# A two-layer transformer trunk on one core: when first weights, a norm, kept weights and projection steps are issued

## The chip, the core and the metric

The kernel runs on one core of a Trainium2 chip. The core has five engines with an instruction stream each: TensorE (PE, matmuls), VectorE (DVE), ScalarE (ACT), GpSimd (POOL) and SyncE (SP); POOL and SP issue nearly all DMAs here. The metric is the device time of one execution in microseconds (us), given as the median of several runs.

## What is computed

The input x has 512 positions of 1024 values. Two layers, each a token mixer and a feed-forward network (FFN), are added to it in turn, each behind an RMS norm, all in float32:

```python
def stick_breaking_mixer(h, w_in, w_out):            # layer 0: 16 heads of 64
    q, k, v = split(h @ w_in, 3)
    z = q k^T / 8;  earlier = key < query
    log_keep = where(earlier, log_sigmoid(-z), 0)
    weight = where(earlier, exp(log_sigmoid(z) + sum of log_keep of later keys), 0)
    return (weight @ v) @ w_out

def diff_mixer(h, positions, w_in, w_out, ...):      # layer 1: 8 heads, q and k 2 x 64, v 128
    q, k, v = split(h @ w_in, 3)
    q, k = rms_norm(q) * q_g, rms_norm(k) * k_g      # per 64 values
    q1, q2, k1, k2 = partial_rope(...)               # the first 16 of 64 values are turned
    a = softmax(mask(q1 k1^T / 8)) - lam * softmax(mask(q2 k2^T / 8))   # mask: chunks of 64
    o = rms_norm(a @ v) * sub_g * (1 - lam_init)
    return o @ w_out

def swiglu_ffn(h, w_gate, w_up, w_down):             # 2816 hidden values
    return (silu(h @ w_gate) * (h @ w_up)) @ w_down
```

## The kernel before

Activations lie transposed, as eight tiles of 128 features by 512 positions (`x[0]` to `x[7]`). To keep float32 accuracy, each matmul operand is split in a rounded part and a rest (`whi`, `wlo` for weights, `hhi`, `hlo` for activations), and each product is three matmuls (`mm3`, L215 to L218). A weight tile of 128x1024 (512 KB) is loaded raw and split by ACT (L109, rounding copy) and DVE (L110, subtraction); in layer 0 a form `wload_acc` is also used, in which POOL's DMA accumulates the rest (`wlo<-in_wv` in the trace).

`stick_layer` is layer 0. It loads q and k weights of its first pair of heads, splits x, computes `ps_q` and `ps_k` of that pair, then the first V block, and goes through eight pairs of heads. `ffn` (L550) is the FFN, in three groups of hidden blocks `f`: gate (`ps_g`) and up (`ps_u`) projections, silu, and `ps_d` for the way down. The norm's factor per position is not applied to its input but behind the matmuls: `norm.finish` sums squares with four small matmuls (`ps_ss`, L190), takes a root on DVE, and in the FFNs spreads the factor over 128 partitions with a matmul (`ps_bc`) and an ACT copy (`rbc`, L213).

While FFN 0 runs, `keep_split` loads the 32 weight tiles of layer 1, splits them and writes both parts back to HBM by POOL's DMAs ("kept" weights), so that layer 1 only loads them. Before, it is called for each hidden block `f` under 20.

`diff_layer` is layer 1. `norm.finish` is called ahead of its first projection. Then it makes chunk 0 of q and k for two heads (`qk_steps`: `ps_nat` of 512 columns, squares, a root, a multiply of the whole 128x2048 chunk at L745, the rotary turn at L762 to L765), `head_stacks` (transposes `tqk` into operands of a head, the halves of k copied by a POOL DMA), and V of chunk 0. Each of the eight heads then calls `attend`: for query tiles 3, 2, 1, 0 `weights` makes two score tiles (`sc`), ACT writes the mask into a 64x64 corner (L786), DVE takes the maximum (L787), ACT the exponential (L788), DVE combines both maps (L800); `wt_bank` transposes the result (`tp`) and splits it (`wt_hi`, `wt_lo`); then `av` is the product with V. `head_out` normalises a head: transposes `tn`, sums of squares on ACT (L835), a root on DVE, four ACT copies with that factor (L850), transposes back (`tb`), a split (`ohi`, `olo`, L857, L858). `out_first` multiplies heads 0 to 3 by the output weights (`ps_o`), `out_second` heads 4 to 7.

The order on each engine is not written out. A scheduler lists the instructions ahead of time from the program's order, which counts as priority, and from its own estimate of when operands are ready. Projections are put between the parts of a head as generators in a queue, the fillers:

```python
def fill(n):                      # n steps of the first generators in the queue
def attend(...):                  # tiles 3 | after, fill | 2 | middle, fill | 1 | fill | 0 | flush
```

`after` is the output of the head before, `middle` makes the next head's stacks. Before, an even head takes the q/k chunk of the next two heads as its filler, an odd head the V chunk, and head 6 and head 7 `out_first`; `flush` empties the queue at each head's end. PSUM has eight banks; `mm` holds two for projections, `scp` the scores, `tnp` the transposes of `head_out`.

Of the kernel before, what the change touches and what calls it, by code (L numbers as in the profile page):

```python
# [43 lines left out]
def trunk(  # L44
# [190 lines left out]
    def flush():  # L235
        while fillers:
            fill(1)
# [46 lines left out]
    def out_second(layer, og, hook, alt):  # L284
# [13 lines left out]
        ws = [out_load(layer, 1, g) for g in range(2)]  # L298
        for g in range(2):
            part(g, ws[g], range(4, 7), False)  # L300
        for g in range(2):
            part(g, ws[g], range(7, 8), True)
        for g in range(2, 4):
            part(g, out_load(layer, 1, g), range(4, 8), True)
# [63 lines left out]
    def attend(tpp, wts, weigh, after, middle, steps):  # L368
        w = [None] * TT
        w[3] = weigh(3)  # L370
        after()
        fill(steps)
        w[2] = weigh(2)
        wt_bank(tpp, wts, w, (2, 3))
        middle()
        fill(steps)
        w[1] = weigh(1)
        wt_bank(tpp, wts, w, (1,))
        fill(steps)
        w[0] = weigh(0)  # L380
        wt_bank(tpp, wts, w, (0,))
        flush()
# [4 lines left out]
    def stick_layer(norm, nxt):  # L387
        h = norm.h
        with ExitStack() as st:
# [7 lines left out]
            first = [wload(wqk0[0])]  # L397
            for i in range(1, 3):
                nc.sync.dma_start(out=x[i], in_=xT[i])
            first.append(wload(wqk0[8]))  # L400
            for i in range(3, KT):
                nc.sync.dma_start(out=x[i], in_=xT[i])
            nc.sync.dma_start(out=gf, in_=g_ffn)
            for i in range(KT):
                norm.scaled(i)
# [11 lines left out]
            def v_chunk(c):  # L417
# [15 lines left out]
                return v, nat_steps([wload_acc(wv0[c, j]) for j in range(2)], h, evac, 256, 1)  # L433
# [14 lines left out]
            pq = mm.tile([P, S], F32, tag="mm", name="ps_q")  # L448
            pk = mm.tile([P, S], F32, tag="mm", name="ps_k")
# [35 lines left out]
            def head(hd, q2, k2, v, after):  # L485
                e = hd % 2
                attend(tpp, wts, lambda qt: weights(q2, k2, e, qt), after, nothing, 1)
# [32 lines left out]
            after = nothing  # L520
            vn = None
            for p in range(8):
                nq = []
                if p < 7:
                    fillers.append(qk_steps(p + 1, nq))
                else:
                    last = out_first(0, og)
                    fillers.append(islice(last, 4))
                o32 = at.tile([P, S], F32, tag="o32", name="o32")
                av = head(2 * p, q2, k2, v, after)  # L530
                after = partial(av_done, 0, av, o32)
                if p == 7:
                    fillers.append(last)
                elif p < 6:
# [3 lines left out]
                av = head(2 * p + 1, q2, k2, v, after)  # L538
                after = partial(pair_done, av, o32)
                if nq:  # L540
                    q2, k2 = nq
# [3 lines left out]
            banks = [(mm, "mm"), (mm, "mm"), (scp, "sc"), (scp, "sc"), (scp, "sc"), (tpp, "tp")]  # L545
            out_second(0, og, nxt.tile_done, banks)

    def ffn(layer, norm, hook, side=None):
        h = norm.h
        with ExitStack() as st:  # L550
# [4 lines left out]
            for j, (f0, nf) in enumerate(THIRDS):  # L555
                a = []
                for f in range(f0, f0 + nf):
# [19 lines left out]
                    if side is not None and f < 20:  # L577
# [109 lines left out]
    def diff_layer(norm, nxt):  # L687
        h = norm.h
        with ExitStack() as st:
# [12 lines left out]
            neg = sm.tile([P, 1], F32, tag="neg", bufs=1, name="neg")  # L702
            V.memset(neg, NEG)
            corner = neg[0:64].to_broadcast([64, 64])
# [4 lines left out]
            def v_chunk(c):  # L709
# [15 lines left out]
                return (vh, vl), nat_steps([wload_kept(("wv", c, j)) for j in range(2)], h, evac, 256, 1)  # L725

            def qk_steps(c, out):
# [3 lines left out]
                def evac(t, ps):  # L731
                    A.activation(t_[:, t], ps, AF.Copy, scale=norm.rstd[:, t : t + 1])
# [45 lines left out]
            def weights(q2, k2, ss, qt):  # L778
# [26 lines left out]
            def head(hh, q2, k2, v, after, middle, steps):  # L805
                ss = sm.tile([P, 2, TT], F32, tag="s12", name="s12")
                attend(tpp, wts, lambda qt: weights(q2, k2, ss, qt), after, middle, steps)
                av = avp.tile([P, S], F32, tag="av", name="av")
# [12 lines left out]
            def head_out(av, ss):  # L821
# [46 lines left out]
            v, steps = v_chunk(0)  # L868
            fillers.append(steps)
            flush()  # L870
            after = nothing
            for hd in range(8):
                hh = hd % 2
                if hd >= 6:
                    if hd == 6:
                        last = out_first(1, og)
                    fillers.append(islice(last, 4) if hd == 6 else last)
                elif hh == 0:
                    fillers.append(qk_steps(hd // 2 + 1, qk))
                else:  # L880
                    vn, steps = v_chunk(hd // 2 + 1)
                    fillers.append(steps)

                def middle():
                    if hd < 7:
                        stacks.append(head_stacks(qk[(hd + 1) // 2], (hd + 1) % 2))

                q2, k2 = stacks[hd]
                av, ss = head(hh, q2, k2, v, after, middle, 2 if hh == 0 and hd < 6 else 1)
                after = partial(head_out, av, ss)  # L890
                if hh == 1 and hd < 7:
# [93 lines left out]
```

## Time and profile before

| | before |
|---|---|
| median of 3 runs | 1269.38 us (1269.35 to 1270.61) |
| the profiled execution | 1275.86 us, span 1274.1 us |
| granted PE clock, mean over the span | 0.98 of full speed |
| PE busy | 1228.4 us, 96% |
| DVE, ACT, POOL busy | 726.1, 585.1, 80.8 us |
| HBM read, written | 154.36, 35.65 MB |

Durations are read from the one profiled execution, so a sum of them is compared with 1275.86 us, not with the median. An engine's busy time is a share over stages with different limits; what a change in one stage is worth is read from that stage. A matmul of 512 columns follows the one before it after 0.23 us at the full clock and after 0.43 us at half.

### The profile page before, as it was taken

To read this page: it belongs to the slowest core of one execution; us is meant where nothing else is said; L and a number is where in the kernel's file an instruction comes from. 1 tells how busy PE (TensorE), PEld (TensorE's weight loads), DVE (VectorE), ACT (ScalarE), POOL (GpSimd) and SP (SyncE) were. 2 spreads that over 40 slices of the span, in tenths; PEclk is the share of its full clock that TensorE was granted. 3 is DMA by queue.
4 is the path that set the end of the run, shared out by engine and by line. 5 is a ranking of instruction groups with operands and counts; after the bars stand their busy time and mean duration, and the time that the engine had idled before them with its cause. 6 is when DMAs were issued, how large, how long until landed. Compare 5 with 4: busy or idle time off the path is not lost.

```text
span 1274.1 us, 15991 instructions
## 1 busy us (share of the span) xinstructions
PE 1228.4 (96%) x5974; PEld 1032.7 (81%) x5974; DVE 726.1 (57%) x1349; ACT 585.1 (46%) x1054; POOL 80.8 (6%) x132
## 2 busy tenths in 40 slices
PE   6999999899999999999999999997899999999998
PEld 4888988777888888888788998776788888888887
DVE  5577777677654655454624776874664434443442
ACT  7788887455332433243414476754442223321220
POOL 1111111001111111100000000000000000000000
PEclk8999999999999999999999999998899999999999
DMA  8766858257777777774735453530233322333222
GB/s 249 189 146 136 190 125 190 66 172 259 243 237 250 248 229 233 243 237 140 272 121 190 153 193 114 174 100 17 100 116 100 95 94 93 100 100 99 95 75 79
DMA packets 60269, 199.44 MB, mean 157 GB/s; under 512 B 8224, under 2 KB 8224, under 8 KB 60192
## 3 DMA queue, kind: packets, MB, share of 16 engines
q1 hardware_dynamic: 41904, 140.74, 34.1%
q0 software_dynamic: 18144, 57.68, 17.0%
q8 instruction: 47, 0.77, 0.2%
q14 instruction: 30, 0.25, 0.1%
q10 hardware_dynamic: 144, 0.01, 0.0%
HBM read 154.36 MB, written 35.65 MB: 149 GB/s over the span
## 4 chain that ended last, share of the span: by engine, by line
PE 87%; issue 6%; DVE 2%; ACT 2%; DMA 2%; POOL 0%; SPq 0%; ACTq 0%; DVEq 0%; POOLq 0%
PE ps_d L218 6%; PE ps_d L216 6%; PE ps_d L217 6%; PE ps_u L216 6%; PE ps_u L218 6%; PE ps_u L217 6%; PE ps_g L217 6%; PE ps_g L218 6%; PE ps_g L216 6%; PE ps_nat L216 5%; PE ps_nat L217 5%; PE ps_nat L218 5%; PE ps_o L216 2%; PE ps_o L217 2%; PE ps_o L218 2%
## 5 line engine op out<-in xcount | busy, mean ns | idle before, releaser
L109 ACT ACTIVATE whi<-wraw 128x1024 fp32r<-128x1024 f32 (+1 forms) x138 | 140.8, 1033 | 359.5 <-PE ps_d L217 79.2
L110 DVE TENSOR_TENSOR wlo<-wraw,whi 128x1024 fp32r<-128x1024 f32 (+1 forms) x138 | 164.4, 1192 | 92.3 <-ACT whi L109 39.2
L216 PE MATMUL ps_u<-hhi,whi 128*128 128x512 f32 x352 | 138.2, 393 | 4.2 <-DVE k L655 2.2
L218 PE MATMUL ps_u<-hhi,wlo 128*128 128x512 f32 x352 | 138.1, 392 | 0.0
L217 PE MATMUL ps_g<-hlo,whi 128*128 128x512 f32 x352 | 138.1, 392 | 0.0
L217 PE MATMUL ps_u<-hlo,whi 128*128 128x512 f32 x352 | 137.9, 392 | 0.0
L216 PE MATMUL ps_g<-hhi,whi 128*128 128x512 f32 x352 | 137.1, 390 | 0.0
L218 PE MATMUL ps_g<-hhi,wlo 128*128 128x512 f32 x352 | 137.0, 389 | 0.0
L217 PE MATMUL ps_d<-alo,whi 128*128 128x512 f32 x352 | 136.6, 389 | 0.0
L218 PE MATMUL ps_d<-ahi,wlo 128*128 128x512 f32 x352 | 136.6, 389 | 0.0
L216 PE MATMUL ps_d<-ahi,whi 128*128 128x512 f32 x352 | 136.4, 389 | 0.0
L216 PE MATMUL ps_nat<-whi,hhi 128*128 128x256 f32 (+1 forms) x384 | 126.7, 330 | 4.7 <-DVE q L309 4.0
L217 PE MATMUL ps_nat<-wlo,hhi 128*128 128x256 f32 (+1 forms) x384 | 125.3, 326 | 2.4 <-DMA wlo<-in_wv 2.4
L218 PE MATMUL ps_nat<-whi,hlo 128*128 128x256 f32 (+1 forms) x384 | 125.0, 326 | 0.0
L586 DVE TENSOR_TENSOR x<-x,ps_d 128x512 f32<-128x512 f32 x48 | 32.7, 685 | 90.8 <-PE ps_d L218 90.8
L216 PEld LDWEIGHTS ps_nat<-whi,hhi 128*128 128x128 f32 x384 | 74.7, 194 | 11.0 <-issue 4.0
L216 PEld LDWEIGHTS ps_u<-hhi,whi 128*128 128x128 f32 x352 | 66.8, 190 | 18.9 <-issue 2.6
L217 PEld LDWEIGHTS ps_nat<-wlo,hhi 128*128 128x128 f32 x384 | 74.7, 194 | 8.0 <-DMA wlo<-in_wv 2.9
L218 PEld LDWEIGHTS ps_nat<-whi,hlo 128*128 128x128 f32 x384 | 74.6, 194 | 4.9
L217 PEld LDWEIGHTS ps_u<-hlo,whi 128*128 128x128 f32 x352 | 66.8, 190 | 14.1 <-DVE hlo L162 0.3
L218 PEld LDWEIGHTS ps_u<-hhi,wlo 128*128 128x128 f32 x352 | 66.7, 190 | 13.9
L217 PEld LDWEIGHTS ps_g<-hlo,whi 128*128 128x128 f32 x352 | 66.2, 188 | 14.2 <-issue 0.5
(205 smaller groups left out, 2326.7 us busy)
## 6 DMA issues: line engine op xcount, KB each, us to landing
wraw<-in_wgu SPq DMA_DIRECT2D x88, 512.0 KB, 3.6
wraw<-in_wd SPq DMA_DIRECT2D x32, 512.0 KB, 3.5
wraw<-in_wqk SPq DMA_DIRECT2D x16, 512.0 KB, 4.7
k<-k POOLq DMA_DIRECT2D x32, 256.0 KB, 3.3
praw<-in_wqk SPq DMA_DIRECT2D x16, 512.0 KB, 5.6
kept_wqk<-whi POOLq DMA_DIRECT2D x16, 512.0 KB, 4.3
kept_wqk<-wlo POOLq DMA_DIRECT2D x16, 512.0 KB, 6.5
whi<-kept_wqk SPq DMA_DIRECT2D x16, 512.0 KB, 5.9
```

The costliest lines, as they stand in the source:

```text
L109: A.activation(hi[:, :cols], raw[:, :cols], AF.Copy)
L110: V.tensor_tensor(lo[:, :cols], raw[:, :cols], hi.bitcast(F32)[:, :cols], op=ALU.subtract)
L216: T.matmul(ps, lh[0], rh[0], start=first, stop=False)
L217: T.matmul(ps, lh[0], rh[1], start=False, stop=False)
L218: T.matmul(ps, lh[1], rh[0], start=False, stop=last)
L586: V.tensor_tensor(x[m], x[m], ps, op=ALU.add)
```

## The change

It has seven parts:

- Start: q and k weights of the first pair are loaded and split in four quarters of 256 columns, between the x tiles, and `ps_q`, `ps_k` lie in the score banks, not in `mm`.
- Layer 0: `attend` takes a number of filler steps for each of its four places, a V chunk is loaded at its first step, `out_first` and the flushes move.
- `out_second`: three pairs of output tiles are begun ahead of the last head, not two, with two more banks in the list.
- FFN 0: kept weights are split and stored from block 2 on, not in blocks 0 to 19.
- Layer 1's norm is finished inside the first projection block's evacuation (`norm_ready`), in the bank `tn`.
- Layer 1: the mask's corner is a DVE memset, the last factor of `head_out` one DVE multiply.
- Layer 1: the q/k and V chunks 1 to 3 are all put in the queue ahead of head 0 and drawn by a table `counts`; a chunk is flushed only where its result is needed.

```diff
+    def flush(upto=None):
+        while fillers and (upto is None or upto in fillers):
...
-        ws = [out_load(layer, 1, g) for g in range(2)]
+        early = range(3)
+        ws = [out_load(layer, 1, g) for g in early]
...
         after()
-        fill(steps)
+        fill(steps[0])
         w[2] = weigh(2)
         wt_bank(tpp, wts, w, (2, 3))
+        fill(steps[1])
         middle()
-        fill(steps)
         w[1] = weigh(1)
         wt_bank(tpp, wts, w, (1,))
-        fill(steps)
+        fill(steps[2])
         w[0] = weigh(0)
         wt_bank(tpp, wts, w, (0,))
-        flush()
+        fill(steps[3])
...
-            first = [wload(wqk0[0])]
...
+            raws = [raw_tile(), raw_tile()]
+            first = [pair(), pair()]
+            for j in range(4):
+                c = slice(j * 256, (j + 1) * 256)
+                for i, (raw, (hi, lo)) in enumerate(zip(raws, first)):
+                    nc.sync.dma_start(out=raw[:, c], in_=wqk0[8 * i][:, c])
...
+                norm.scaled(2 * j)
+                for raw, (hi, lo) in zip(raws, first):
+                    A.activation(hi[:, c], raw[:, c], AF.Copy)
+                    V.tensor_tensor(lo[:, c], raw[:, c], hi.bitcast(F32)[:, c], op=ALU.subtract)
+                norm.scaled(2 * j + 1)
...
-            pq = mm.tile([P, S], F32, tag="mm", name="ps_q")
-            pk = mm.tile([P, S], F32, tag="mm", name="ps_k")
+            pq = scp.tile([P, S], F32, tag="sc", name="ps_q")
+            pk = scp.tile([P, S], F32, tag="sc", name="ps_k")
...
-                    if side is not None and f < 20:
+                    if side is not None and f > 1:
                         keep_split(rawp, *side[1].pop(0))
...
-            norm.finish(mm, "mm")
-            V.tensor_scalar_mul(rsv, norm.rstd, phi)
+            def norm_ready():
+                if not norm.done:
+                    norm.finish(tnp, "tn")
+                    V.tensor_scalar_mul(rsv, norm.rstd, phi)
...
                 def evac(t, ps):
+                    norm_ready()
...
-                    A.activation(ps[0:64, n - 64 : n], corner, AF.Copy)
+                    V.memset(ps[0:64, n - 64 : n], NEG)
...
-                for t in range(TT):
-                    c = slice(t * P, (t + 1) * P)
-                    A.activation(on[:, c], tp[:, c], AF.Copy, scale=u[:, t : t + 1])
+                V.tensor_tensor(
+                    on.rearrange("p (t d) -> p t d", d=P),
+                    tp.rearrange("p (t d) -> p t d", d=P),
+                    u.unsqueeze(2).to_broadcast([P, TT, P]),
...
+            for c in range(1, 4):
+                gens["qk", c] = qk_steps(c, qk)
+                gens["v", c] = v_steps(c, vs)
+                fillers.extend((gens["qk", c], gens["v", c]))
+            last = out_first(1, og)
+            counts = ((2, 1, 2, 1), (2, 1, 1, 1)) * 3 + ((1, 1, 1, 1), (1, 1, 1, 1))
...
                     if hd < 7:
+                        if hh == 1:
+                            flush(gens["qk", c + 1])
...
+                def before():
+                    if c > 0:
+                        flush(gens["v", c])
+                    if hd == 6:
+                        fillers.append(last)
```

How the listed order moves, at three places (a name's number is its buffer; what an instruction waits for stands in brackets: an engine, `DMAHW` for a load by SP's queue, `DMASW` for a DMA of POOL).

PE, between FFN 0's last matmuls (`ps_d`) and layer 1's first (`ps_nat`), before:

```order
L217 MATMUL ps_d_5586<-alo_5311,whi_5572 128x512
L218 MATMUL ps_d_5586<-ahi_5310,wlo_5573 128x512
L190 MATMUL ps_ss_5654<-ones_98,ssum_5344 128x1 [waits DVE_49]
L190 MATMUL ps_ss_5654<-ones_98,ssum_5344 128x1 x3
L216 MATMUL ps_nat_5694<-whi_5678,hhi_5340 128x512 [waits DMAHW0_49]
L217 MATMUL ps_nat_5694<-wlo_5679,hhi_5340 128x512 [waits DMAHW1_49]
```

and now, at the place where the norm's matmuls (`ps_ss`) stand:

```order
L216 MATMUL ps_nat_5688<-whi_5684,hhi_5624 128x512 [waits Activation_49]
L217 MATMUL ps_nat_5688<-wlo_5685,hhi_5624 128x512
L218 MATMUL ps_nat_5688<-whi_5684,hlo_5625 128x512 [waits DVE_49]
L190 MATMUL ps_ss_5713<-ones_98,ssum_5362 128x1 [waits DVE_49,PE_49]
L190 MATMUL ps_ss_5713<-ones_98,ssum_5362 128x1 x3
L218 MATMUL ps_nat_5739<-whi_5676,hlo_5475 128x512
```

The norm's matmuls stood right behind `ps_d`; now 35 matmuls of the first two projection blocks stand between.

ACT, ahead of FFN 0's first silu, before (`whi` is a split of a weight, of a kept one where it is from `praw` or its buffer is given back by a POOL DMA):

```order
L109 ACTIVATE whi_3172<-wraw_3171 128x1024 [waits DMAHW1_49,PE_49]
L109 ACTIVATE whi_3203<-wraw_3202 128x1024 [waits DMAHW2_49,DMASW4_49,DVE_49]
L109 ACTIVATE whi_3244<-praw_3243 128x1024 [waits DMAHW0_49,PE_49]
L213 ACTIVATE rbc_2907<-ps_bc_2905 128x512 [waits PE_49]
L568 ACT_TABLE_LOAD
L568 ACTIVATE g32_2909<-g32_2909 128x512 [waits DVE_49]
```

and now:

```order
L109 ACTIVATE whi_3172<-wraw_3171 128x1024 [waits DMAHW5_49,PE_49]
L109 ACTIVATE whi_3203<-wraw_3202 128x1024 [waits DMAHW6_49,DMASW0_49,DVE_49]
L213 ACTIVATE rbc_2925<-ps_bc_2923 128x512 [waits PE_49]
L109 ACTIVATE whi_3244<-praw_3243 128x1024 [waits DMAHW4_49,PE_49]
L588 ACT_TABLE_LOAD
L588 ACTIVATE g32_2927<-g32_2927 128x512 [waits DVE_49]
```

Of the two splits ahead of `rbc`, the one that waits for a POOL DMA still stands there; one of a kept weight now stands behind it.

PE, at the first scores of layer 1's head 6 (`sc`, ahead of them the q and k stacks' transposes `tqk`), before:

```order
L218 MATMUL ps_o_8244<-ohi_7246,wlo_8201 128x512
L355 MATMUL tp_7766<-ident_93,e1_7531 128x128 [waits DVE_49]
L355 MATMUL tp_7766<-ident_93,e1_7622 128x128
L355 MATMUL tp_7766<-ident_93,e1_7696 128x128
L355 MATMUL tp_7766<-ident_93,e1_7748 128x128
L774 MATMUL tqk_7921<-ident_93,qk_nat_7250 128x128 [waits DVE_49]
L774 MATMUL tqk_7921<-ident_93,qk_nat_7250 128x128 x3
L216 MATMUL ps_o_8324<-ohi_7590,whi_8316 128x512 [waits DMAHW1_49,DVE_49,Activation_49]
L217 MATMUL ps_o_8324<-olo_7591,whi_8316 128x512
L218 MATMUL ps_o_8324<-ohi_7590,wlo_8317 128x512 [waits DMAHW0_49]
L337 MATMUL sc_7817<-k2_7661,q2_7651 128x512 [waits DMASW2_49]
```

and now:

```order
L218 MATMUL ps_o_8330<-ohi_7499,wlo_8309 128x512
L798 MATMUL tqk_7610<-ident_93,qk_nat_7279 128x128 [waits DVE_49]
L798 MATMUL tqk_7610<-ident_93,qk_nat_7279 128x128 x3
L856 MATMUL tn_7784<-ident_93,wraw_7780 128x128 [waits Activation_49]
L856 MATMUL tn_7784<-ident_93,wraw_7780 128x128 x3
L798 MATMUL tqk_7620<-ident_93,qk_nat_7279 128x128 [waits DVE_49,PE_49]
L798 MATMUL tqk_7620<-ident_93,qk_nat_7279 128x128 x3
L883 MATMUL tb_7813<-ident_93,wraw_7780 128x128 [waits DVE_49,Activation_49]
L883 MATMUL tb_7813<-ident_93,wraw_7780 128x128 x3
L798 MATMUL tqk_7901<-ident_93,qk_nat_7279 128x128 [waits DVE_49,PE_49]
L798 MATMUL tqk_7901<-ident_93,qk_nat_7279 128x128 x3
L340 MATMUL sc_7764<-k2_7625,q2_7615 128x512 [waits DMASW2_49,Activation_49]
```

Before, output matmuls (`ps_o`, 81 of them between head 5's first scores and these) stand up to the stacks; now the output of head 5 (`tn`, `tb`) and the stacks stand alone, and 6 of the 81 are left in that stretch. On DVE, the multiply of the whole q/k chunk for heads 6 and 7 stood among head 5's first maxima,

```order
L148 SCALAR_TENSOR_TENSOR rs_u_7483<-rs_t_7484,rs_u_7483 128x32 [waits DVE_49]
L359 TENSOR_TENSOR wt_lo_5648<-tp_7392,wt_hi_5647 128x384 [waits Activation_49]
L745 TENSOR_TENSOR qk_nat_7250<-qk_nat_7250,rs_u_7483 128x2048 [waits DVE_49]
L858 SCALAR_TENSOR_TENSOR olo_7247<-tb_7241,gs_105,ohi_7246 128x512 [waits Activation_49]
L796 RECIPROCAL c_7545<-s12_7529 128x1 [waits Activation_49]
L359 TENSOR_TENSOR wt_lo_5648<-tp_7446,wt_hi_5647 128x512 [waits Activation_49]
L787 TENSOR_REDUCE nm_7621<-sc_7624 128x1 [waits Activation_49]
L787 TENSOR_REDUCE nm_7621<-sc_7630 128x1 [waits Activation_49]
```

and now it stands behind the last of them, ahead of head 5's last `wt_lo`:

```order
L873 TENSOR_TENSOR rs_u_7480<-rs_u_7480,fin_7476 128x4 [waits DVE_49]
L147 TENSOR_TENSOR rs_t_7588<-rs_t_7588,qk_ss_7280 128x32 [waits DVE_49]
L874 TENSOR_TENSOR wraw_7461<-tn_7465,rs_u_7480 128x512 [waits DVE_49]
L148 SCALAR_TENSOR_TENSOR rs_u_7587<-rs_t_7588,rs_u_7587 128x32 [waits DVE_49]
L769 TENSOR_TENSOR qk_nat_7279<-qk_nat_7279,rs_u_7587 128x2048 [waits DVE_49]
L362 TENSOR_TENSOR wt_lo_5666<-tp_7713,wt_hi_5665 128x512 [waits Activation_49]
L887 SCALAR_TENSOR_TENSOR olo_7500<-tb_7494,gs_105,ohi_7499 128x512 [waits Activation_49]
L786 TENSOR_TENSOR rope_7600<-qk_nat_7279,rot01_101 128x16x8 [waits DVE_49]
```

so that the turn (`rope`) and the stacks of head 6 follow head 5's whole softmax.

## Rows read from the trace of the kernel before

**Rows 1.** The page: busy time of each engine, and the chain that ended last.
```profile
PE 1228.4 (96%) x5974; PEld 1032.7 (81%) x5974; DVE 726.1 (57%) x1349; ACT 585.1 (46%) x1054; POOL 80.8 (6%) x132
...
PE 87%; issue 6%; DVE 2%; ACT 2%; DMA 2%; POOL 0%; SPq 0%; ACTq 0%; DVEq 0%; POOLq 0%
```

**Rows 2.** Waits of PE: line, releaser; us in total, times, longest us.
```profile
PE tb L854 <- ACT wraw L850: 6.8, 1, 6.8
...
PE ps_nat L216 <- DVE q L309: 4.0, 1, 4.0
PE ps_ss L190 <- DVE ssum L177: 2.9, 1, 2.9
...
PE ps_u L216 <- ACT g L568: 2.0, 1, 2.0
```

**Rows 3.** Table by stretches: from:to, length, busy us of each engine (instructions), clock, DMA, GB/s.
```profile
45.00:200.00 155.00, 155.00 (x931) 137.66 (x930) 117.49 (x195) 129.63 (x232) 26.15 (x33) 1.00 0.72 161
302.00:316.00 14.00, 12.01 (x44) 9.15 (x43) 10.41 (x20) 8.60 (x11) 1.06 (x2) 0.88 0.77 269
765.20:795.60 30.40, 30.40 (x177) 26.55 (x176) 20.63 (x55) 18.54 (x53) 1.16 (x2) 1.00 0.37 103
814.00:845.60 31.60, 29.28 (x154) 23.59 (x153) 26.66 (x77) 17.64 (x57) 1.16 (x2) 1.00 0.39 128
845.60:857.80 12.20, 9.04 (x46) 7.13 (x44) 10.70 (x34) 9.75 (x36) 1.16 (x2) 0.88 0.22 43
857.80:881.30 23.50, 19.87 (x84) 15.15 (x85) 14.46 (x50) 14.35 (x51) 0.00 (x0) 0.77 0.03 9
881.30:896.80 15.50, 7.97 (x41) 6.40 (x39) 3.53 (x17) 4.87 (x15) 0.00 (x0) 0.86 0.14 55
```

**Rows 4.** Timeline of PE, 20 to 27 us: start, us, instruction [idle before <- releaser].
```profile
20.05 0.95 PE L190 MATMUL ps_ss<-ones,ssum 128*128 128x1 f32 x8
24.95 0.36 PE L216 MATMUL ps_nat<-whi,hhi 128*128 128x256 f32 x1 [3.96 <-DVE q L309]
26.77 0.58 PE L217 MATMUL ps_nat<-wlo,hhi 128*128 128x256 f32 x1 [1.46 <-DMA wlo<-in_wv]
```

**Rows 5.** Timeline of ACT, 303 to 306 us.
```profile
303.94 1.06 ACT L109 ACTIVATE whi<-wraw 128x1024 fp32r<-128x1024 f32 x1 [3.99 <-DMA kept_wqk<-whi]
...
305.97 0.60 ACT L213 ACTIVATE rbc<-ps_bc 128x512 f32<-128x512 f32 x1
```

**Rows 6.** Timeline of PE, 633 to 641 us.
```profile
633.64 0.39 PE L217 MATMUL ps_d<-alo,whi 128*128 128x512 f32 x1
633.87 0.39 PE L218 MATMUL ps_d<-ahi,wlo 128*128 128x512 f32 x1
637.18 1.86 PE L190 MATMUL ps_ss<-ones,ssum 128*128 128x1 f32 x8 [2.92 <-DVE ssum L177]
...
639.91 0.63 PE L218 MATMUL ps_nat<-whi,hlo 128*128 128x512 f32 x1
640.33 0.63 PE L216 MATMUL ps_nat<-whi,hhi 128*128 128x512 f32 x1
```

**Rows 7.** DVE, groups by form: xcount | busy us, mean ns | idle before <- releaser.
```profile
L745 DVE TENSOR_TENSOR qk_nat<-qk_nat,rs_u 128x2048 f32<-128x2048 f32 x3 | 6.9, 2284 | 0.0
...
L281 DVE TENSOR_TENSOR x<-x,ps_o 128x512 f32<-128x512 f32 x8 | 5.4, 682 | 3.8 <-PE ps_o L218 3.8
...
L96 DVE MEMSET ones<- 128x128 f32 x1 | 0.2, 165 | 0.0
```

**Rows 8.** ACT, groups by form, 694 to 912 us.
```profile
L786 ACT ACTIVATE sc<-neg 64x64 f32<-64x64 f32 x64 | 13.5, 217 | 23.5 <-PE sc L338 23.1
...
L850 ACT ACTIVATE wraw<-tn,rs_u 128x128 f32<-128x128 f32 x32 | 9.1, 365 | 7.0 <-DVE rs_u L847 7.0
```

**Rows 9.** DMA issues of 694 to 912 us: xcount, KB each, median us to landing.
```profile
k<-k POOLq DMA_DIRECT2D x14, 256.0 KB, 3.2
```

**Rows 10.** Timeline of DVE, 890 to 892 us, ahead of `tb`.
```profile
890.78 1.23 DVE L110 TENSOR_TENSOR wlo<-wraw,whi 128x1024 fp32r<-128x1024 f32 x1
```

More of the change, by code (lines that the diff above doesn't have):

```diff
@@ L233, in fill @@
                 fillers.popleft()
-    def flush():
-        while fillers:
-            fill(1)
+    def flush(upto=None):
+        while fillers and (upto is None or upto in fillers):
+            try:
+                next(fillers[0])
+            except StopIteration:
+                fillers.popleft()
     def gemm_steps(ps, w, h, n=2):
@@ L296, in part @@
                     hook(m)
-        ws = [out_load(layer, 1, g) for g in range(2)]
-        for g in range(2):
+        early = range(3)
+        ws = [out_load(layer, 1, g) for g in early]
+        for g in early:
             part(g, ws[g], range(4, 7), False)
-        for g in range(2):
+        for g in early:
             part(g, ws[g], range(7, 8), True)
-        for g in range(2, 4):
-            part(g, out_load(layer, 1, g), range(4, 8), True)
+        part(3, out_load(layer, 1, 3), range(4, 8), True)
     def split(out_hi, out_lo, src, gain, hi):
@@ L431, in evac, with steps @@
                     )
-                return v, nat_steps([wload_acc(wv0[c, j]) for j in range(2)], h, evac, 256, 1)
+                def steps():
+                    yield from nat_steps(
+                        [wload_acc(wv0[c, j]) for j in range(2)], h, evac, 256, 1
+                    )
+                return v, steps()
             def k_stack(ps):
@@ L483, in weights, with head @@
                 return w
-            def head(hd, q2, k2, v, after):
+            def head(hd, q2, k2, v, after, steps):
                 e = hd % 2
-                attend(tpp, wts, lambda qt: weights(q2, k2, e, qt), after, nothing, 1)
+                attend(tpp, wts, lambda qt: weights(q2, k2, e, qt), after, nothing, steps)
                 av = avp.tile([P, S], F32, tag="av", name="av")
@@ L520, in stick_layer @@
             after = nothing
+            last = out_first(0, og)
             vn = None
@@ L524, in stick_layer @@
                 if p < 7:
[L525 to L534, printed above, removed]
+                    qk_gen = qk_steps(p + 1, nq)
+                    fillers.append(qk_gen)
+                if p < 6:
                     if p % 2 == 0:
@@ L537, in stick_layer @@
                     fillers.append(islice(steps, 2))
-                av = head(2 * p + 1, q2, k2, v, after)
+                if p == 7:
+                    fillers.append(last)
+                o32 = at.tile([P, S], F32, tag="o32", name="o32")
+                av = head(2 * p, q2, k2, v, after, (1, 1, 1, 1))
+                if p < 7:
+                    flush(qk_gen)
+                after = partial(av_done, 0, av, o32)
+                av = head(2 * p + 1, q2, k2, v, after, (1, 0, 1, 0))
                 after = partial(pair_done, av, o32)
+                if p < 7:
+                    flush()
                 if nq:
@@ L723, in evac @@
                     )
-                return (vh, vl), nat_steps([wload_kept(("wv", c, j)) for j in range(2)], h, evac, 256, 1)
+                out.append((vh, vl))
+                yield from nat_steps(
+                    [wload_kept(("wv", c, j)) for j in range(2)], h, evac, 256, 1
+                )
             def qk_steps(c, out):
@@ L803, in weights, with head @@
                 return e1
-            def head(hh, q2, k2, v, after, middle, steps):
+            def head(hh, q2, k2, v, after, middle, steps, before):
                 ss = sm.tile([P, 2, TT], F32, tag="s12", name="s12")
                 attend(tpp, wts, lambda qt: weights(q2, k2, ss, qt), after, middle, steps)
+                before()
+                v = v()
                 av = avp.tile([P, S], F32, tag="av", name="av")
```

45 lines of the change are left out of this document (18 added, 27 removed).

## Prediction

> **What bounds the kernel now.** I read first the busy shares and the chain of work that ended last [rows 1]. TensorE (PE) is busy 96% of the span and holds 87% of the chain. So a change pays where PE idles or runs at its lower clock, and costs where it opens such a place. Second, PE's waits [rows 2]: those touched here are 6.8 us ahead of `tb` (end of the last layer-1 head), 4.0 us ahead of the first V block, 2.9 us ahead of `ps_ss` (layer 1's norm) and 2.0 us in FFN 0. Third, the table by stretches [rows 3]. From 45 to 200 us, most of layer 0's attention, PE fills 155.00 of 155.00 us: a more even spread of projection steps finds nothing to fill there. In layer 1, heads 4 and 5 (765 to 846 us) leave PE almost no idle time, while the last two heads and the end (845.6 to 896.8) have 37 us of PE in 51, partly at a granted clock of 0.77, a mixture of 1.2 and 2.4 GHz.
>
> **Start.** The diff frees PE from 3.96 us behind the split of head 0's q [rows 4]. But one matmul into the first V block PE waits for its accumulated weights, which let it go on at 26.77 [rows 4]. In the new order the raw V tiles come free only behind the fourth quarter, so these weights land later: what is late next is this DMA. ACT also pays: four splits of a quarter instead of one of 1024 columns (1.06 us [rows 5]) carry four fixed costs. I take **0**, bounds 3 us gained (the wait goes, V weights hold) to 3 us lost (V a few us later).
>
> **Layer 0's body and its output.** 0 us: PE is full in the body [rows 3]. In the output stage PE's instruction order is the same before and after, since the scheduler already ran three pairs ahead, so the third `early` pair and two more PSUM banks only say what happened anyway. Bounds: 2 us either way.
>
> **FFN 0's first blocks.** Storing kept weights from f = 2 takes two splits and four DMA writes of 512 KB out of the time before the norm's broadcast. ACT waits 3.99 us for such a write and only then copies `rbc` [rows 5], for which PE waits 2.0 us [rows 2]; the stretch around it has a granted clock of 0.88 [rows 3]. At 0.88 some 24% of 12.0 busy us ran at 1.2 GHz, which loses half, 1.4 us. Gain **3.4**, bounds 0 (`rbc` still stands behind one split that waits for a store) to 5.
>
> **Layer 1's norm behind its first block.** Before: 2.92 us idle, eight small matmuls in 1.86 us, and then matmuls 0.43 us apart against 0.23 ahead of the gap [rows 6], for nine matmuls up to 643 us, which cost 1.85 us. After: 35 projection matmuls stand ahead of `ps_ss`, whose input is long ready then. Gain 2.92 + 1.85 + 0.93 (half of 1.86) = **5.7**, bounds 3 (a kept weight lands late) to 6.5.
>
> **Corner and normalisation from ACT to DVE.** Removed: 64 ACT writes of 217 ns [rows 8], 13.5 us, and 32 of 365 ns, 9.1 us [rows 8]. Added on DVE: 64 memsets of 64x64 in PSUM and eight multiplies of 128x512, near 0.69 us like the additions of that size [rows 7]. No row shows this memset. The nearest are a memset of 128x128 in SBUF at 165 ns [rows 7] and ACT's write of the same 64x64 at 217 ns [rows 8]; with half the columns of the first, on the same engine, I take 130 ns, and the ends are 83 (half of 165) and 217. That is 1.0 us of DVE per head against 1.7 us of ACT and one crossing between engines for each score tile. Where PE is covered this costs nothing; in uncovered heads more DVE time and the saved crossing cancel: **0**, bounds 3 us either way. A page would make it dearer: the Trainium skill, "Perfetto Trace Analysis", section "Optimizing Scalar/DVE Operations", puts the fixed access cost in PSUM at about 125 ns for DVE and 51 ns for ScalarE, which speaks against this move; by it the memset is an estimated 0.19 us, three uncovered heads lose 1.5 us, and the sum below would be 6.8. No row before has a DVE memset in PSUM.
>
> **Fillers of layer 1.** This is the large term. All q/k and v chunks are queued ahead, and the order shows where PE's work goes. From head 5's first scores to head 6's, before, PE has 81 output matmuls, in all 29.28 us of work in 31.60 us, beside 26.66 us of DVE [rows 3]. After, only 6 of the 81 are left; the others stand before head 5's scores. What stays is two heads' scores, transposes and products: 12.4 us at 0.227 us per 512 columns [rows 6], less for fewer. DVE's work stays: 26.66, less six additions of 0.68 [rows 7], plus the second head output and eight memsets, 24 to 27 us; its order also puts the 2.28 us multiply of the last q/k chunk [rows 7] behind head 5's softmax, so that head 6's stacks come last. Then the copy of k takes 3.2 us to land [rows 9]. So about 28 us pass, 15.6 idle for PE, against 2.3 before; of this 1 us comes back in the next stretch, which no longer holds head 5's product. Cost **+12**, bounds 3 (ACT and DVE overlap better than in order) to 18. Head 3's stretch gets the same tail of chunk 2: the matching stretch before is 30.40 us, all PE, DVE 20.63 [rows 3]. After, PE has 27.5 us there, DVE 101 instructions, some 28 us, and the copy of k: **+4**, bounds 0 and 10. Heads 6 and 7 were uncovered before and stay so: 0.
>
> **The last head.** A weight split of 1.23 us lay inside DVE's chain to `tb` [rows 10]; it now stands ahead of it. One multiply of 0.69 replaces four ACT copies of 365 ns [rows 8]. Gain **1.6**, bounds 0 and 3.
>
> **Sum:** 0 + 0 − 3.4 − 5.7 + 0 + 12 + 4 − 1.6 = +5.3 us. The profiled execution took 1275.86 us, 1.8 more than its span; the sum makes that 1281.2. It lies 6.5 above the median of the runs, 1269.38, so the forecast is 1274.7, given as 1275.
>
> **Rivals.** (a) *The cover holds: faster.* If DVE and ACT overlap in heads 3 and 5 so that no more than 4 us are lost, the three gains decide: 1269.4 − 3.4 − 5.7 − 1.6 + 4 = about 1262.7, and 1258 with none lost. The point is at 10.7 us of new idle time in heads 3 and 5. For it: in the uncovered stretch after 857.8, DVE has only 14.46 us in 23.5 [rows 3], so much of that time is crossings, one of which the change removes for each tile. Against it: 26.66 us of DVE in head 5's stretch and 12.4 of PE. Chance 0.35.
> (b) *Uncovered heads fall to 1.2 GHz.* The granted clock was 0.77 in the stretch with 3.6 us idle in 23.5 [rows 3]; with 15 us idle in head 5's stretch all its 12.4 us of PE could run at 1.2 GHz, and what follows too, 12 us more: 1287. For it: the same rows. Against: a wait for DVE hides a slow PE in part. Chance 0.12. The Trainium skill, "TensorE: Matmul & The Clock Gate", section "HAM oscillation — how this bites in real kernels", says that a loop whose matmuls are parted by waits restarts at the low clock again and again and should be arranged to keep PE fed; the rows at 0.77 agree.
> (c) *Even.* The start loses or FFN 0's gain fails, and head 5 costs 6 us instead of 12: within 2.5 us of 1269.4. Chance 0.13.
> (d) *It doesn't do what it says:* `rbc` still waits for a store and FFN 0 gains nothing: 1278. It is a part of the forecast's case.
>
> **Numbers.** Forecast's own case, 1272 to 1282: 0.40; (a) 0.35; (b) 0.12; (c) 0.13. A change of 0.2%, 2.5 us, is about what a measurement of this kernel can tell. The range reaches from 1258, (a) with nothing lost, to 1288, (b). Faster 0.35, within 0.2% 0.13, slower 0.52. Between the two large cases, the likeliest one gives the time.
>
> **What would show it.** Right: in PE's waits `ps_ss` of layer 1 and `ps_u` of FFN 0 are gone or under 1 us; no 0.43 us matmuls after 634 us; PE full up to head 5's first scores, later than before by some 15 us relative to the layer's start, then 12 us of PE in 25 to 30, with waits for DVE ahead of `av`, `tqk` and `sc`. Wrong: if PE's idle time in heads 3 and 5 together is under 10 us, the kernel is faster and (a) holds; if V's weights land after 30 us, the start's term has failed.

## The result, and the profile after

| | before | after |
|---|---|---|
| median | 1269.99 us (1269.35 to 1270.97, 4 runs) | 1301.17 us (1300.61 to 1304.95, 4 runs) |
| ratio | | 1.0251, 95% interval 1.0230 to 1.0272 |
| span of the profiled execution | 1274.1 us | 1299.6 us |

The change makes the kernel 31 us slower. Slower was the likeliest case of the prediction, but 1301 lies outside its range of 1258 to 1288. The two profiled executions are 25.5 us apart and the medians 31: the profiled execution of before lies 6 us above its median, that of after does not.

The page's busy times and chain after, to set beside [rows 1]:

```profile
PE 1239.7 (95%) x5974; PEld 1032.3 (79%) x5974; DVE 740.2 (57%) x1426; ACT 568.2 (44%) x964; POOL 80.8 (6%) x132
...
PE 90%; DVE 3%; ACT 3%; DMA 2%; issue 1%; SPq 0%; POOL 0%; DVEq 0%; ACTq 0%; POOLq 0%
```

PE executes the same number of instructions. It is busy 11 us longer, for reasons that follow (the lower clock in layer 1, slower matmuls in the FFNs), and idle 14 us longer. The waits of PE after, to set beside [rows 2] (line, releaser; us in total, times, longest):

```profile
PE sc L340 <- ACT e L812: 11.1, 13, 3.1
PE tb L883 <- DVE wraw L874: 8.2, 5, 4.7
PE ps_nat L217 <- DMA wlo<-in_wv: 7.0, 1, 7.0
...
PE tp L358 <- DVE wt_lo L362: 4.7, 4, 1.6
PE tqk L798 <- DVE q L315: 3.4, 1, 3.4
```

`ps_ss` (2.9) and FFN 0's `ps_u` (2.0) are gone from the list, as forecast. The first V block's wait is not gone: 4.0 for a split became 7.0 for a DMA. And waits inside layer 1's heads have grown: `tqk` is new, `tp` for `wt_lo` was 1.7, and `sc` for an exponential was, before,

```profile
PE sc L337 <- ACT e L788: 5.5, 5, 2.2
```

Layer 1 by stretches, first scores of heads 3 to 4, 5 to 6, 6 to 7, and head 7 to its product, to set beside [rows 3] (columns as there):

```profile
778.70:819.00 40.30, 32.67 (x199) 27.98 (x198) 30.95 (x103) 20.28 (x56) 1.16 (x2) 0.87 0.37 131
840.90:873.90 33.00, 20.15 (x89) 14.84 (x89) 25.84 (x96) 15.78 (x49) 1.16 (x2) 0.78 0.04 9
873.90:886.00 12.10, 8.89 (x36) 6.50 (x36) 10.13 (x29) 7.03 (x19) 1.16 (x2) 0.88 0.33 64
886.00:903.30 17.30, 14.29 (x66) 10.17 (x66) 13.38 (x56) 9.42 (x32) 0.00 (x0) 0.90 0.00 1
```

Head 3's stretch took 30.40 us before, all of it PE, and takes 40.30 now; head 5's took 31.60 with 29.28 us of PE and takes 33.00 with 20.15, at a granted clock of 0.78. Head 6's is as before (12.20); head 7's is shorter (23.50 before, with 84 matmuls where it now has 66). From head 0's first scores to FFN 1 layer 1 takes 242 us instead of 216.

The norm's place after, PE at the end of FFN 0 and at `ps_ss`, beside [rows 6]:

```profile
634.51 0.40 PE L218 MATMUL ps_d<-ahi,wlo 128*128 128x512 f32 x1
634.74 0.39 PE L216 MATMUL ps_nat<-whi,hhi 128*128 128x512 f32 x1
...
642.47 0.39 PE L218 MATMUL ps_nat<-whi,hlo 128*128 128x512 f32 x1
642.70 0.95 PE L190 MATMUL ps_ss<-ones,ssum 128*128 128x1 f32 x8
```

No gap and no matmul 0.43 us apart. FFN 0's first blocks, beside the row of the same stretch in [rows 3]:

```profile
302.00:316.00 14.00, 14.00 (x61) 11.23 (x61) 10.78 (x15) 10.03 (x14) 1.06 (x2) 1.00 0.75 251
```

PE is full there, at the full clock. The start, beside [rows 4]:

```profile
20.42 0.39 PE L216 MATMUL ps_nat<-whi,hhi 128*128 128x256 f32 x2
27.79 0.58 PE L217 MATMUL ps_nat<-wlo,hhi 128*128 128x256 f32 x1 [6.98 <-DMA wlo<-in_wv]
```

The V weights let PE go on 1.0 us later than before, and the first scores come at 45.1 us instead of 43.8. The operations that moved to DVE, beside [rows 7, 8]:

```profile
L810 DVE MEMSET sc<- 64x64 f32 x64 | 7.1, 112 | 24.7 <-PE sc L341 23.6 <-ACT wraw L850 0.2
...
L874 DVE TENSOR_TENSOR wraw<-tn,rs_u 128x512 f32<-128x512 f32 x8 | 5.5, 689 | 0.2
```

The memset takes 112 ns where the estimate was 130.

One group of rows shows what nobody looked for. The way down of both FFNs, which the diff does not touch, after and then before, from the page's groups (xcount | busy us, mean ns of one):

```profile
L217 PE MATMUL ps_d<-alo,whi 128*128 128x512 f32 x352 | 139.1, 396 | 0.0
```

```profile
L217 PE MATMUL ps_d<-alo,whi 128*128 128x512 f32 x352 | 136.6, 389 | 0.0
```

and three of these matmuls in FFN 1 after:

```profile
1280.20 0.40 PE L217 MATMUL ps_d<-alo,whi 128*128 128x512 f32 x1
1280.44 0.39 PE L218 MATMUL ps_d<-ahi,wlo 128*128 128x512 f32 x1
1280.67 0.40 PE L216 MATMUL ps_d<-ahi,whi 128*128 128x512 f32 x1
```

They start 0.235 us apart at a granted clock of 1.00 (the mean of one is 7 ns up, 396 against 389); before it was 0.227, as `ps_g` and `ps_u` still have. With 1056 such matmuls this is some 7 us, in two stages that the change leaves alone.

### The profile page after: what moved, and what is told of

Read it like the earlier page. It is cut to its first block, busy times and chain, and to the rows that moved or that the text cites. A ratio compares the mean times of both kernels' runs of the same rounds, so it can differ in the third digit from the quotient of the medians.

```text
span 1299.6 us, 16000 instructions
## 1 busy us (share of the span) xinstructions
PE 1239.7 (95%) x5974; PEld 1032.3 (79%) x5974; DVE 740.2 (57%) x1426; ACT 568.2 (44%) x964; POOL 80.8 (6%) x132
## 4 chain that ended last, share of the span: by engine, by line
PE 90%; DVE 3%; ACT 3%; DMA 2%; issue 1%; SPq 0%; POOL 0%; DVEq 0%; ACTq 0%; POOLq 0%
PE ps_d L217 6%; PE ps_d L216 6%; PE ps_d L218 6%; PE ps_g L218 6%; PE ps_g L216 6%; PE ps_g L217 6%; PE ps_u L218 6%; PE ps_u L216 6%; PE ps_u L217 6%; PE ps_nat L216 4%; PE ps_nat L217 4%; PE ps_nat L218 4%; PE ps_o L216 2%; PE ps_o L217 2%; PE ps_o L218 2%; PE tp L358 2%
## 5 line engine op out<-in xcount | busy, mean ns | idle before, releaser
L217 PEld LDWEIGHTS ps_d<-alo,whi 128*128 128x128 f32 x352 | 66.2, 188 | 15.9
L218 PEld LDWEIGHTS ps_d<-ahi,wlo 128*128 128x128 f32 x352 | 66.2, 188 | 15.9
L216 PEld LDWEIGHTS ps_d<-ahi,whi 128*128 128x128 f32 x352 | 66.2, 188 | 15.9
```

The lines of the kernel that those rows point to most:

```text
L216: T.matmul(ps, lh[0], rh[0], start=first, stop=False)
L217: T.matmul(ps, lh[0], rh[1], start=False, stop=False)
L218: T.matmul(ps, lh[1], rh[0], start=False, stop=last)
```

## The experiments

Ratios are to runs of the kernel before on the same chip, with 95% intervals; its median there was 1271.5 to 1272.1 us.

**What layer 1 pays for.** Two explanations stood: the queue (the rest of a q/k chunk now comes behind the odd head's softmax), and the load that moved to DVE.

```diff
# e1: changed kernel, in before()
+                    if hh == 0 and hd < 6:
+                        flush(gens["qk", c + 1])
# e2: kernel before, layer 1's queue alone
-                elif hh == 0:
-                    fillers.append(qk_steps(hd // 2 + 1, qk))
...
+                fillers.extend((gens["qk", c], gens["v", c]))
...
+                            flush(gens["qk", c + 1])
# e3: changed kernel, corner (and the four copies of head_out) back on ACT
-                    V.memset(ps[0:64, n - 64 : n], NEG)
+                    A.activation(ps[0:64, n - 64 : n], corner, AF.Copy)
# e4: kernel before, the reverse of e3
-                    A.activation(ps[0:64, n - 64 : n], corner, AF.Copy)
+                    V.memset(ps[0:64, n - 64 : n], NEG)
```

> The changed kernel with one more flush: an even head ends with the rest of the next q/k chunk, as before the change, instead of the odd head's middle. Theory Q (the tail of the q/k chunk behind the odd head's softmax costs layer 1 its 27 us): layer 1's heads go back to what they took, 216 us from the first scores to FFN 1, and the kernel comes to 1270 - 5.5 (norm) - 3 (FFN 0) + 1.3 (start) = 1263, between 1259 and 1268. Rival D (corner and last factor on DVE slow each head): it stays above 1285.

Measured 1271.28 us, ratio 0.9993 (0.9980 to 1.0006). One flush takes back 2.6%. From layer 1's first projections to head 7's softmax its listed order on PE is that of e10 below, which has the whole old scheme of fillers. The stretches of heads 3 and 5 there:

```profile
759.90:794.70 34.80, 34.80 (x212) 30.98 (x211) 25.28 (x77) 17.30 (x43) 1.16 (x2) 1.00 0.48 151
811.30:841.60 30.30, 28.18 (x143) 22.41 (x144) 27.37 (x83) 12.47 (x37) 1.16 (x2) 1.00 0.38 122
```

PE is full in the first and 28 of 30 us in the second, at the full clock, with nearly as much DVE work in the two as in the changed kernel (25.28 and 27.37 us against 30.95 and 25.84). The 1263 that was expected was missed by 8 us; the fifth run accounts for 7 of them.

> The kernel before with nothing of the change but layer 1's queue: chunks queued ahead, the table of steps, the flush in the odd head's middle. Corner and factor stay on ACT. Theory Q: 1270 + 27 = 1297, between 1291 and 1303, with 10 us or more of PE idle in heads 3 and 5 each. Rival D: 1267 to 1275.

Measured 1310.97 us, ratio 1.0306 (1.0285 to 1.0328): the queue alone costs 39 us where corner and factor stay on ACT, more than the 21 to 33 expected. PE idles 12.8 us in head 3 and 12.3 in head 5 there, as Theory Q said.

> The changed kernel with the corner and the last factor back on ACT. Theory Q: within 4 us of the changed kernel's 1301. Rival D: 1285 or less.

Measured 1304.53 us, ratio 1.0253 (1.0232 to 1.0273), as the changed kernel's 1.0251. Its FFNs are faster, though, for the reason that e4 brings up, so in layer 1 it loses more than the changed kernel does.

> The kernel before with the corner as a DVE memset and the last factor as one DVE multiply, nothing else. Theory Q: within 3 us of 1270, and a memset takes 0.11 us. Rival D: 1280 or more.

Measured 1276.21 us, ratio 1.0034 (1.0018 to 1.0051). DVE's load is not the cause of the 31 us. But 4 us more were not expected, and its trace shows the slow `ps_d` matmuls, as e1's does, while e2 and e3 have them 0.227 apart. The kernels with slow ones are those without the constant tile `neg` of the corner, 4 bytes per partition; in the program's memory plan the activation tiles of the FFNs (`ahi` and `alo` among them) then lie 32 bytes lower, the weights where they were.

**The moved tiles.**

```diff
# e5: the kernel of e1, and e6: the kernel before, both ahead of rsv
+            pad = sm.tile([P, 1], F32, tag="pad", bufs=1, name="pad")
+            V.memset(pad, 0.0)
```

> The kernel of the first experiment (changed kernel, rest of the q/k chunk flushed at the even head's end) with one unused tile of 4 bytes per partition, which puts every SBUF tile of the FFNs back where it lay before the change, 32 bytes higher. Theory S (without the tile of the corner's constant the FFN tiles moved by 32 bytes, and the 1056 matmuls of the way down, 0.232 to 0.235 us apart in place of 0.227, lose 7 us): matmuls of ps_d 0.227 apart again, 7 us off both FFNs, the kernel about 1264, ratio 0.993 to 0.996 to the kernel before. Rival C (those matmuls are slow because of something in the new instruction stream): no change, ratio 0.999.

> The kernel before with one unused tile of 4 bytes per partition and one memset, nothing else: the FFN's tiles move 32 bytes the other way. Theory S: matmuls of ps_d 0.232 to 0.235 us apart, 7 us more, ratio 1.005. Rival C: ratio 1.000.

Measured 1263.23 us, ratio 0.9940 (0.9927 to 0.9953) for the fifth, and 1279.79, ratio 1.0067 (1.0053 to 1.0081) for the sixth: an unused tile of 4 bytes takes 7 us off one kernel (e5 against e1) and puts 8 on the other. Two more runs ask whether a tile's own place counts, or its place against others:

```diff
# e13: the kernel before with pad and a second tile pad2 like it
# e14: the kernel before, ahead of the first constants
+    pad = const.tile([P, 1], F32, name="pad")
+    V.memset(pad, 0.0)
```

> The kernel before with two unused tiles of 4 bytes per partition ahead of the FFN tiles, which move 64 bytes up. If the place within 64 bytes decides: matmuls of ps_d 0.227 us apart, ratio 1.000. If any place but the old one is slow: 0.232 to 0.235, ratio 1.006.

> The kernel before with one unused tile of 4 bytes per partition at the lower end, so that every later tile, inputs and weights too, moves 32 bytes up. If the place of activations against weights decides: ps_d 0.227 us apart, ratio 1.000. If a tile's own place decides: also ps_g, ps_u and ps_nat 0.232 to 0.235 apart, and 25 us or more above.

e13: 1275.48 us, ratio 1.0027 (1.0015 to 1.0039), between the two forecasts. e14: 1272.32 us, ratio 0.9999 (0.9984 to 1.0013). Matmuls of the way down in FFN 1, one group of e6 (its other two are alike), the three of e13, and the first of e14 (whose line numbers are two higher; its others are alike):

```profile
L216 PE MATMUL ps_d<-ahi,whi 128*128 128x512 f32 x176 | 69.2, 395 | 0.0
```

```profile
L216 PE MATMUL ps_d<-ahi,whi 128*128 128x512 f32 x176 | 69.0, 394 | 0.0
L218 PE MATMUL ps_d<-ahi,wlo 128*128 128x512 f32 x176 | 68.8, 392 | 0.0
L217 PE MATMUL ps_d<-alo,whi 128*128 128x512 f32 x176 | 68.2, 388 | 0.0
```

```profile
L218 PE MATMUL ps_d<-ahi,whi 128*128 128x512 f32 x176 | 68.1, 389 | 0.0
```

Where everything moves by 32 bytes nothing slows, where only the upper tiles move by 32 all three products slow, and where they move by 64 one slows, one a little, one not. So the place of the activations (`ahi`, `alo`) against the tiles below them, weights among these, counts, not their own; which pairs meet how is open.

**The other parts, one at a time.** Each is put into the kernel before.

```diff
# e7
-            norm.finish(mm, "mm")
...
+                    norm_ready()
# e8
-            first = [wload(wqk0[0])]
...
+            raws = [raw_tile(), raw_tile()]
...
-            pq = mm.tile([P, S], F32, tag="mm", name="ps_q")
+            pq = scp.tile([P, S], F32, tag="sc", name="ps_q")
# e9
-                    if side is not None and f < 20:
+                    if side is not None and f > 1:
```

> The kernel before with layer 1's norm inside the first block's evacuation, nothing else. By the prediction's step 5.7 us less; by the two traces 5: ratio 0.996. A rival, that the norm's root on DVE then delays the first blocks: within 0.998 to 1.000.

Measured 1263.86 us, ratio 0.9940 (0.9922 to 0.9957), some 2 us more gain than expected. In its trace layer 1's first scores come 54.9 us after FFN 0's last `ps_d`, 60.4 before: 5.5 us of the gain lie where the norm stood, and where the other 2 lie is open.

> The kernel before with the new start (quarters, ps_q and ps_k in the score banks), nothing else. By the traces of the changed kernels so far, where the first scores come 1.3 to 3 us later, the V weights land later by more than the wait that goes: 1.5 to 3 us more, ratio 1.001 to 1.002. Rival (the wait of 3.96 us goes and nothing follows): 2 to 4 us less, ratio 0.997 to 0.998.

Measured 1271.71 us, ratio 1.0004 (0.9994 to 1.0013): no change, between the two forecasts.

> The kernel before with kept weights stored from block 2 on, nothing else. By the prediction's step 3.4 us less; by the FFN 0 times of the traces so far (360 to 361 us with it, 361 to 364 without) 1 to 3: ratio 0.9975 to 0.999. Rival, that the later stores delay layer 1's or FFN 0's loads: 1.000 or more.

Measured 1269.29 us, ratio 0.9984 (0.9973 to 0.9995): a small gain of 2 us.

**Together.** e10 is the kernel before with the edits of e7, e4 and the pad; e11 adds that of e9; e12 is e5 without that of e8.

> The kernel before with the norm behind the first block, corner and last factor on DVE, and the unused tile of 4 bytes that leaves the FFN tiles where they were. If the parts add: 0.994 (norm) times 1.0034 less the 7 us of the shifted tiles (0.9975): ratio 0.9915, 1261. Rival, that the corner's move gains nothing once the shift is taken out: 0.994.

Measured 1268.34 us, ratio 0.9974 (0.9962 to 0.9986): above both forecasts. With the norm alone it was 0.9940, so here the corner's move costs 4 us, while in e4, less the 7 us of moved tiles, it gained 3. In the traces the two part at the end: from head 7's first scores to FFN 1, e4 takes 46.1 us at a granted clock of 0.89, e10 52.2 at 0.80, and e7, without the corner's move, 49.0 at 0.84. (These are single executions: e4's lies 3 us under its median, e10's 2 above.)

> As the run before, and kept weights stored from block 2 on. If the store's move gains by itself, 1 to 3 us below the run before; rival, that with the norm moved the later stores and loads meet, 2 to 4 us above it.

Measured 1264.50 us, ratio 0.9944 (0.9928 to 0.9961): 4 us below e10, in the first forecast's direction and a little beyond its 1 to 3.

> The kernel of the fifth experiment with the start as before the change; against the run before it has in addition only the new places of filler steps in layer 0 and three pairs ahead. By the start alone (ratio 1.0004) as the fifth, 0.994; if layer 0's new places cost nothing, equal to the run before within 0.001.

Measured 1264.32 us, ratio 0.9945 (0.9928 to 0.9962), as e11 and e5: layer 0's new filler places and the third early pair cost and gain nothing that is measured.

**Why the late tail costs so much.** In the changed kernel 11 us pass between the last turn of the last chunk and head 6's first score, with the q and k stacks one after the other in one PSUM bank. e15 and e16 give the k stack a bank of `mm`, in the changed kernel and in e5:

```diff
-                    tp = tqp.tile([P, S], F32, tag="tq", name="tqk")
+                    pool, tag = ((tqp, "tq"), (mm, "mm"))[which]
+                    tp = pool.tile([P, S], F32, tag=tag, name="tqk")
```

> The changed kernel with the transposes of the k stack in a bank of mm, so that q and k stacks no longer wait for each other; the listed order then has head 0's scores 24 us of PE work earlier and 20 to 28 us of PE work between the first scores of any two heads up to head 6. Theory chain (the serial stacks make heads wait and let the fillers run out): layer 1 loses 20 us or more, 1275 to 1282 with the shifted FFN tiles. Rival (DVE's time and the late tail alone): within 6 us of the changed kernel, 1295 or more.

> The fifth experiment's kernel (rest of the chunk flushed at the even head's end, FFN tiles in their old place) with the k stack in a bank of mm. Theory chain: between first scores stand 19 to 32 us of PE work everywhere, so the 20 us that heads 5 to 7 still lose in the fifth go down to under 8: 1263 - 12 = 1251, ratio 0.98 to 0.987. Rival: as the fifth, 0.994.

Measured 1302.93 us, ratio 1.0247 (1.0228 to 1.0267), and 1272.95, ratio 1.0014 (1.0003 to 1.0025). Neither run gained what the theory asked for, and e16 came out 9 us slower than e5, outside both forecasts. But the edit did not test the bank alone: in both lists head 0's stacks now stand ahead of V's projections, and PE waits there for the turn of chunk 0, which it does in neither e5 nor the changed kernel (e16; e15 has the same 8.9):

```profile
PE tqk L801 <- DVE qk_nat L791: 8.9, 1, 8.9
```

Less this wait, by estimate, e16 is as e5, where the theory said 12 us less, and e15 some 9 us below the changed kernel, where it said 20 or more. So the one bank is not the main cause; a part of the loss it may be. Heads 1, 3 and 5 of e15, from first scores to first scores:

```profile
703.20:736.20 33.00, 27.24 (x166) 23.62 (x165) 23.65 (x82) 16.22 (x48) 1.16 (x2) 0.84 0.43 144
759.10:794.40 35.30, 28.17 (x156) 23.86 (x156) 24.71 (x84) 17.59 (x51) 1.16 (x2) 0.81 0.40 134
815.60:856.00 40.40, 32.73 (x180) 27.70 (x179) 28.26 (x98) 19.76 (x56) 1.16 (x2) 0.87 0.35 118
```

PE idles 6 to 8 us in each odd head, at a granted clock of 0.81 to 0.87, though it has 27 to 33 us of work (at that clock) in each stretch. Work somewhere in the stretch does not cover a wait; it must stand in PE's order ahead of the instruction that waits.

## Why the prediction was right and wrong

**Right: the places, the direction and the idle time.** PE idles in heads 3 and 5, behind waits of `sc`, `tp`, `tqk` and `av`; e1 and e2, two opposite edits, put the loss on the queue, and e3 and e4 clear DVE's load of it.

**Wrong: the size of the fillers' term.** The step gave +12 for head 5 and +4 for head 3, all of it idle time of PE. The flush of e1 is worth 2.58% of 1270, 33 us, and from head 0's first scores to FFN 1 the traces of the changed kernel and of e1 differ by 30, with the same 1111 matmuls:

```profile
689.46:931.80 242.34, 208.81 (x1111) 173.69 (x1110) 165.30 (x516) 114.83 (x306) 8.11 (x14) 0.92 0.36 116
688.80:901.10 212.30, 195.83 (x1111) 166.96 (x1110) 160.70 (x515) 113.22 (x304) 8.11 (x14) 0.97 0.41 133
```

PE is idle 33.5 us in the first and 16.5 in the second: 17 of the 30 us are idle time, near the 16 of the step. The other 13 are the same matmuls taking longer, at a mean granted clock of 0.92 against 0.97. This is what the step left out: it priced the time in which PE stands still and not the slower clock that came with it. How the idle time arises it had only in part, as the first two points show.

First, head 3 was priced by totals: 27.5 us of PE work against some 28 of DVE. It idles 7.6 us, where +4 was forecast and PE was to be full up to head 5's scores. DVE's count was near (30.95 us), but PE's fillers stood in its order behind head 3's product, and the waits ahead of it. PE in the changed kernel, head 3's last two query tiles:

```profile
789.36 0.44 PE L358 MATMUL tp<-ident,e 128*128 128x128 f32 x2
792.87 0.58 PE L340 MATMUL sc<-k,q 128*128 128x256 f32 x1 [3.08 <-ACT e L812]
...
795.26 0.47 PE L358 MATMUL tp<-ident,e 128*128 128x128 f32 x1 [0.74 <-DVE e L824]
797.12 0.48 PE L358 MATMUL tp<-ident,e 128*128 128x128 f32 x1 [1.38 <-DVE wt_lo L362]
```

and what ACT did in the 3.08 us for which PE waited for an exponential to give back a score bank:

```profile
790.83 0.64 ACT L758 ACTIVATE qk_sq<-qk_nat 128x512 f32<-128x512 f32 x1
791.35 0.50 ACT L361 ACTIVATE wt_hi<-tp 128x384 fp32r<-128x384 f32 x1
791.72 0.65 ACT L758 ACTIVATE qk_sq<-qk_nat 128x512 f32<-128x512 f32 x1
792.24 0.49 ACT L812 ACTIVATE e<-sc,nm 128x256 f32<-128x256 f32 x1
```

Two squares of the q/k chunk (`qk_sq`, some 1 us) and, ahead of them, those of head 2's output stand before the exponential at 792.24. The tail is late not only on DVE: its ACT part sits in the odd head's chain too. The prediction named what is queued on DVE and left ACT out.

Second, for head 5 the step put 3.2 us between the last stack and head 6's scores. PE and DVE there:

```profile
864.10 0.60 PE L798 MATMUL tqk<-ident,qk_nat 128*128 128x128 f32 x4
864.53 0.60 PE L856 MATMUL tn<-ident,wraw 128*128 128x128 f32 x4
868.54 0.63 PE L798 MATMUL tqk<-ident,qk_nat 128*128 128x128 f32 x4 [3.41 <-DVE q L315]
871.85 1.09 PE L883 MATMUL tb<-ident,wraw 128*128 128x128 f32 x4 [2.68 <-DVE wraw L874]
...
873.87 0.77 PE L340 MATMUL sc<-k,q 128*128 128x512 f32 x1
```

```profile
861.97 0.76 DVE L789 TENSOR_TENSOR qk_nat<-rope 128x256 f32<-128x256 f32 x2
865.45 0.74 DVE L315 SCALAR_TENSOR_TENSOR q<-tqk,gqT,q 64x512 fp32r<-64x512 f32 x1 [2.72 <-ACT q L314]
```

From the end of the turn (862.7) to the score (873.9) it is 11 us: the q stack, its split, the k stack, its split, with head 5's own output (`tn`, `tb`) between on all three engines. 28 us were forecast for the stretch, 33.00 came; yet PE's idle time in it, 12.9 us, is under the 15.6 of the step, and its matmuls took 20.15 us where 12.4 were counted. That the delay is a chain of small shares on three engines and not the one bank is read from these rows; e15, whose edit also moved other work, does not show it by itself.

Third, and this is the largest part of the miss, rival (b) came beside the forecast's case and not in its place. The granted clock was 0.87 and 0.78 in the two stretches, 1.00 in both in e1. The rule of the Trainium skill that was set beside this rival ("TensorE: Matmul & The Clock Gate", "HAM oscillation — how this bites in real kernels") agrees with these clocks. By the prediction's way of reckoning 26% of 32.67 us and 44% of 20.15 ran at 1.2 GHz, which loses 4.2 and 4.4 us; by the same estimate 0.92 against 0.97 over all of the heads is some 11 of the 13 us. The rival had put this loss at 12 us, with a chance of 0.12, as a case of its own; it belonged into the sum.

**Wrong: nothing for the corner's move.** The memset was well priced (112 ns, 130 forecast). The estimate of 190 ns from the Trainium skill ("Perfetto Trace Analysis", "Optimizing Scalar/DVE Operations") was too high: the trace has 112. But the diff also deletes the tile `neg`, and no step asked what a deleted tile moves. e5 and e6 show 7 and 8 us for it, outside the term's bounds of 3 either way. What is left of the corner by itself has no one sign: 3 us gained in e4 and 4 lost in e10, whose lists differ around head 7's product, which was not tried apart. With the new queue it gains: e3, with corner and factor on ACT, takes as long as the changed kernel although its FFNs are 7 us faster, and its layer 1, from the first scores to FFN 1, takes 251 us against 242.

**Nearly right: the small terms.** Norm: −5.7, e7 measured −7.6, a little beyond the bound of 6.5, of which its trace places 5.5 at the norm; the wait and the half clock are gone in the rows. Kept weights: −3.4, e9 measured −2.0, within the bounds. Start: 0, e8 measured +0.5 of 1271; its argument, that the DMA of V's weights is late next, is in the row at 27.79. Layer 0: 0, as e11 and e12 show. The last head: −1.6; `tb` still waits 4.7 us at the end against 6.75, 2.0 less. No run has this part alone.

With the measured sizes the sum is 33 + 7 − 7.6 − 2 + 0.5 = 31, beside 31 measured. The corner by itself and the last head are not in it, and the terms come from different kernels, so that it comes out to the microsecond is in part luck: e5, the changed kernel without the late flush and the moved tiles, measured −7.6 where the last three terms give −9.1. Rival (a) had its deciding point at 10.7 us of new idle time in heads 3 and 5, and the rows show 18 (7.6 and 12.9 us, against 0 and 2.3 before).

## What to carry to other kernels

Two totals over a stretch, PE's work and another engine's, do not say how much of one hides the other: read in the listed order whether the filler stands ahead of the instruction that waits, and follow the chain on every engine that it crosses. Where a change opens idle time on PE, put the slower matmuls around it into the same sum and not into a rival: here 17 us of idle time came with 13 of these. In a queue of generators the place where a generator is forced to its end sets the priority of its last, non-matmul part; here one such line is worth 33 us, and the version with it, the pad and the rest of the change (e5) beats both kernels at 0.9940, no better than the norm's move alone. When a diff deletes a small tile, look at what stands above it in SBUF.

## What the runs showed of the hardware

Matmuls of 512 columns with the same shapes, data and granted clock took 0.227 us apart or 0.232 to 0.235, depending on 32 bytes in the place of their moving operand against tiles below it; moving everything by 32 bytes changed nothing, moving the upper tiles by 64 slowed one of the three products and a second a little. This cost 0.5 to 0.7% of the kernel, and an unused 4-byte tile turned it on (e6) or off (e5). A DVE memset of 64x64 in PSUM took 112 ns, against 217 ns of ACT's write of the same corner.
